# Attention step of a hybrid encoder layer: scores of a head pair as one group on eight PSUM banks, transposes in the pair's own step

## The chip, the cores and the metric

One NeuronCore of a Trainium2 chip. The time is the device time of the whole program in microseconds. The kernel before took 524.53 us (median of three runs, 524.23 to 525.28).

## What is computed

One encoder layer on 512 positions of width 1024. After an input projection one half of the mix is a gated linear recurrence, the other is attention with eight heads of 64 columns, and both are normed, projected out, and followed by an MLP. The change touches the attention:

```python
def dilated_attention(q, k, v, rel_bias):
    ...
        for offs, bias in pats:
            kpos = pos[:, None] + offs[None, :]
            ...
            logits = jnp.einsum('bqhd,bqjhd->bhqj', qb, kg).astype(jnp.float32) * scale
            logits = logits + bias[None, :, None, :]
            lse = jax.nn.logsumexp(logits, axis=-1)
            p = jnp.exp(logits - lse[..., None])
            outs.append(jnp.einsum('bhqj,bqjhd->bqhd', p.astype(v.dtype), vg).astype(jnp.float32))
            lses.append(lse)
        w = jax.nn.softmax(jnp.stack(lses, axis=0), axis=0)
        ...
        o = jnp.sum(w * jnp.stack(outs, axis=0), axis=0)
    ...
mix = jnp.concatenate([rms_norm(y_rnn, norm_rnn_g[l]), rms_norm(y_attn, norm_attn_g[l])], axis=-1)
x = x + mix @ w_out[l]
```

The kernel folds the three windows into one softmax: their multiplicities are logarithms inside the bias.

## The kernel before

Every float32 product is three products of split operands (`mm3`, lines 312 to 314), so a projection over 512 columns is one matmul after another with no pause. The program fixes the order on TensorE, ScalarE, VectorE and GpSimd by hand: an engine runs its instructions in the order in which the code emits them. SyncE (the queue SP) issues most transfers in order too; within the attention loop its order is also the code's.

The heads are worked in four pairs. For a pair and each of four query blocks `u`: `att_s` (line 806) makes the scores of both heads, each over 64 rows of the array, into one PSUM bank per head; `att_e` adds the bias and takes the minimum on VectorE (line 822; the bias windows `tw` are loaded by `load_tw`) and exponentiates on ScalarE (line 823); `att_t` transposes three 128x128 blocks per head and key block on TensorE (line 842) into a bank of the kind "et", which ScalarE copies out (line 845), and `att_c` transposes the small corner on VectorE. `att_z` takes the reciprocals of the row sums, writes them to DRAM (`zd`), and `att_zd` reads them back spread over 128 partitions (`zrow`). `att_av` (line 942) multiplies with the values over 64 columns of the array, and VectorE's `yp` (line 948) evacuates the sum, times `zrow`.

PSUM has eight banks: four "pj", two "gs", two "et". Between these pieces `fill(1)` emits one thunk: three matmuls of the query and key projections (`pqk`), later of the output projection (`pwo`). A thunk also carries the split of the next weights (`conv_hi`, line 247, `whi`; `conv_lo`, line 269, `wlo`, after which the next weight load `wraw` is issued). `beside` places side work by the table `plan`: the recurrence's end, norms, splits of queries and keys (`qh`, `kk`), and the sums and splits for the output projection (`osum`, `oh`, `ol`).

Before the change the loop has five steps `i` of four `u`. In step `i` the scores of pair `i` stand in two groups of 12 matmuls, and the transposes are those of pair `i - 1`; the value products stand at (2, 2) for pair 0, at (4, 0) for pairs 1 and 2, and behind the loop for pair 3. The step (4, 0) also loads the table for the square root (`act(warm, epsb, AF.Sqrt)`).

Of the kernel before, what the change touches and what calls it, by code (L numbers as in the profile page):

```python
# [17 lines left out]
P = 128  # L18
# [80 lines left out]
def hybrid_kernel(ctx: ExitStack, tc, xw0, xw, xn, w_in, w_v, w_out, w_up, w_dn, gates, vecs, bias, fg, out):  # L99
# [19 lines left out]
    def ps_(name, tag):  # L119
        return psum.tile([P, S], FT, name=name, tag=tag, bufs={"pj": 4, "gs": 2, "et": 2}[tag])  # L120
# [674 lines left out]
    QT = ((1, 0), (1, 1), (0, 0), (0, 1))  # L795
    QSEQ = (0, 3, 1, 2)

    def att_s(p, us):
        for u in us:
            psq[p, u] = [ps_("ps", "pj" if u % 2 else "gs") for _ in range(2)]  # L800
        for i, (a, b) in enumerate(((0, 0), (0, 1), (1, 0))):
            for u in us:
                qt = QSEQ[u]
                w = {(0, 0): TH + TH - WN, (0, 1): 0, (1, 0): TH - WN, (1, 1): TH}[QT[qt]]
                for e, r in enumerate(halves):
                    nc.tensor.matmul(psq[p, u][e][:, :NK], lhsT=qs_[p, a][r, P * qt:P * qt + P], rhs=kks[p][r, b, w:w + NK], start=i == 0, stop=i == 2)  # L806

    def att_e(p, u):
        qt = QSEQ[u]
# [71 lines left out]
    def att_y(p):  # L881
        y_add(1)
# [49 lines left out]

    def att_av(p, jts):
        if 0 in jts:
            pav[p] = ps_("pav", "gs" if p else "pj")
        for jt in jts:
            parts = av_parts(jt)
            for i, (ci, co) in enumerate(parts):
                for e in range(2):
                    a = slice(64 * e, 64 * e + 64)  # L940
                    h = 2 * p + e
                    nc.tensor.matmul(pav[p][a, co], lhsT=vs[:, jt, h * DH:(h + 1) * DH], rhs=et[h, jt][:, ci],  # L942
                                     start=jt == 0 and i == 0, stop=jt == 3 and i == len(parts) - 1, skip_group_check=True)
            for e in range(2):
                del et[2 * p + e, jt]
        if 3 in jts:
            y = g_("yp")
            nc.vector.tensor_tensor(y[:, ::-1], pav.pop(p), zrow.pop(p), op=OP.mult)
            yat[p] = y
            if p == 3:  # L950
                att_a(p)
            if p != 2:
                att_q(p)
            if p < 2:
                att_a(p)

    def att_q(p):
        y_sq(yat[p], 1)
# [1 line left out]
    def att_a(p):  # L960
        at[p] = g_("at")
        act(at[p], yat[p], AF.Copy, scale=vec("yg", 4 + p))
# [18 lines left out]
    def wo_thunks():  # L981
        order = [(0, tt, k) for tt in range(4) for k in range(4)] + [(1, tt, k) for h in (0, 2) for tt in range(4) for k in (h, h + 1)]
        pw = {}

        def end(n, tt):
            stt(x1[tt, n], pw[n, tt], rc[0][:, tt:tt + 1], x1[tt, n], op0=OP.mult, op1=OP.add)

        def mk(b, n, tt, k):
            def run():
                if k == 0:  # L990
                    pw[n, tt] = ps_("pwo", "pj")
                o = pw[n, tt]
# [7 lines left out]
                if n == 0 and tt and k == 1:  # L1000
                    end(0, tt - 1)
# [5 lines left out]
        st["wo"] = lambda tt: end(1, tt)  # L1007
        return [mk(b, *o) for b, o in enumerate(order)]

    KSPLIT = {7: s_hi, 8: s_lo}  # L1010
# [27 lines left out]
    def load_x():  # L1038
# [12 lines left out]
        def w_in(t, b):  # L1051
            return lambda: nc.sync.dma_start(t, oblock(b))
# [50 lines left out]
    def op(fn, *a):  # L1103
        return lambda: fn(*a)


    plan = {(0, 0, 0): [end(0)], (0, 0, 2): [sq_(0), add], (0, 0, 3): [end(1)],
            (0, 1, 1): [sq_(1)],
            (0, 2, 3): [add],
            (1, 0, 2): [end(2)],  # L1110
            (1, 1, 0): [sq_(2)], (1, 1, 2): [end(3)], (1, 1, 4): [add],
            (1, 3, 0): [sq_(3)], (1, 3, 2): [hi(0)], (1, 3, 3): [add, hi(1)], (2, 0, 2): [rnn_cols],
            (2, 0, 0): [lo(0), lo(1)], (2, 0, 4): [hi(2)],
            (2, 1, 2): [hi(3)], (2, 1, 4): [lo(2)], (2, 2, 3): [lo(3)]}
    for i in range(3):
        for key, (is_k, fn) in {(0, 2): (0, s_hi), (1, 0): (0, s_lo), (2, 2): (1, s_hi), (3, 0): (1, s_lo)}.items():
            plan.setdefault((i,) + key, []).append(lambda fn=fn, a=(i + 1, is_k): fn(*a))

    def beside(*key):
# [7 lines left out]
        fill(1)  # L1127
    assert not scans

    for key, fs in (((4, 1, 2), [(att_a, 2), (o_sum, "s1", 0), (o_sum, "s2", 0), (o_sum, "s3", 0), (o_sum, "s3", 1), (o_sum, "22", 0)]),  # L1130
                    ((4, 2, 0), [(o_hi, "s2", 0), (o_hi, "11", 0)]), ((4, 2, 2), [(o_lo, "s2", 0), (o_lo, "11", 0)]),
                    ((4, 3, 0), [(att_q, 2), (o_hi, "11", 1), (o_hi, "s3", 0), (o_hi, "s3", 1)]), ((4, 3, 2), [(o_lo, "11", 1), (o_lo, "s3", 0)]),
                    ((4, 3, 4), [(att_y, 2), (o_lo, "s3", 1), (o_hi2, 0), (o_hi, "s1", 0), (o_hi, "22", 0)])):
        plan[key] = [op(*a) for a in fs]
    FILL = {(3, 0): (1, 1, 1, 0), (3, 1): (1, 1, 1, 0), (3, 2): (1, 1, 1, 0), (4, 0): (0, 1, 0, 0), (4, 1): (0, 1, 0, 1), (4, 2): (0, 1, 0, 0), (4, 3): (0, 1, 0, 0)}


    AVS = {(2, 2): (0,), (4, 0): (1, 2)}
    with tc.manual_schedule(engines={nc.sync.engine}):
        for i in range(5):  # L1140
            for u in range(4):
                if i < 4:
                    if i == 2 and u == 2:
                        att_av(0, range(4))
                    if u % 2 == 0:
                        att_s(i, (u, u + 1))
                    if u == 2 and i < 3 or u == 0 and i:
                        for e in range(2):
                            load_tw(2 * (i + u // 2) + e, u // 2)
                if i >= 1:  # L1150
                    att_t(2 * i - 2, u)
                    att_t(2 * i - 1, u)
                if i < 4:
                    att_e(i, u)
                if i >= 1:
                    att_c(2 * i - 2, u)
                    att_c(2 * i - 1, u)
                if u == 0 and i >= 1:
                    att_z(i - 1)
                for p in AVS.get((i, u), ()) if i == 4 else ():  # L1160
                    att_av(p, range(4))
                if (i, u) == (4, 0):
                    act(warm, epsb, AF.Sqrt)
                beside(i, u, 0)
                fill(FILL.get((i, u), (1, 1, 1, 1))[0])
                beside(i, u, 1)
                fill(FILL.get((i, u), (1, 1, 1, 1))[1])
                if u == (1 if i == 4 else 2) and i >= 1:
                    att_zd(i - 1)
                for p in AVS.get((i, u), ()):  # L1170
                    if p != 2:
                        att_y(p)
                beside(i, u, 2)
                fill(FILL.get((i, u), (1, 1, 1, 1))[2])
                beside(i, u, 3)
                fill(FILL.get((i, u), (1, 1, 1, 1))[3])
                add_x()
                beside(i, u, 4)
    assert not plan and not more

    def load_t(half, n, f0):
        t = work.tile([P, 1024], FT, name="tw", tag="tw", bufs=4)
# [41 lines left out]
        nc.vector.tensor_tensor(hb["l"][k], hm[k], f(hb["h"])[:, k, :], op=OP.subtract)  # L1224

    fill(1)
    conv_lo(C_WA + 2)
    att_av(3, range(4))
    fill(1)
    o_sum("s1", 1)  # L1230
    o_sum("s2", 1)
    o_hi("s2", 1)
    remake(C_WA + OSEQ.index("s4"))
    fill(1)
    att_y(3)
# [13 lines left out]
    def rc_neg():  # L1249
        nc.vector.tensor_scalar(nrc, rc[1], -1.0, None, op0=OP.mult)  # L1250

    BES["11"].update({1: lambda: (o_lo("s2", 1), o_hi2(1), remake(C_WA + OSEQ.index("s1"))), 3: lambda: (rc_neg(), st["wo"](2))})
    BES["s2"].update({1: lambda: (o_lo2(0), conv_lo(C_WA + 3)), 2: lambda: o_hi("s1", 1), 3: lambda: (conv_lo(C_WA + 4), o_lo2(1))})
    BES["s3"][3] = lambda: (conv_lo(C_WA + 5), st["wo"](3))
# [570 lines left out]
```

## Time and profile before

| quantity | value |
|---|---|
| median of the runs | 524.53 us |
| the profiled execution | 524.5 us, its span 522.7 us |
| TensorE busy | 516.4 us, 99% |
| VectorE, ScalarE, GpSimd busy | 82%, 67%, 12% |

The profiled execution's span is 1.8 us shorter than its time; the prediction is made against its time. TensorE's granted clock is at full speed in all 40 slices. The chain that ended last is TensorE alone (99%). So a microsecond on TensorE, a pause or a slower stretch, is a microsecond of the kernel.

### The profile page before, as it was taken

The page shows a single profiled execution, that of the slowest core. Times are in us where ns is not written, and L with a number is a line of the kernel's source. Part 1 is how long each engine was busy: PE and PEld are TensorE (multiplying, and loading weights), DVE is VectorE, ACT ScalarE, POOL GpSimd, SP SyncE. Part 2 cuts the span into 40 slices and gives each one's busy share as a digit, 9 for nine tenths or more (in the row PEclk, how much of TensorE's full clock was granted, in tenths as well). Part 3 has the DMA queues.
Part 4 walks back from the last instruction along what each step waited for, and adds up shares of the span by engine and source line. Part 5 has one row for each costly group of instructions (what it writes and reads, how often), then busy time and mean ns, then how long its engine had stood idle before and what let it go on. Part 6 is the DMA issues. An engine that isn't in the chain of part 4 may idle for free.

```text
span 522.7 us, 8216 instructions
## 1 busy us (share of the span) xinstructions
PE 516.4 (99%) x3021; PEld 443.6 (85%) x3021; DVE 430.2 (82%) x667; ACT 352.7 (67%) x571; POOL 65.3 (12%) x89
## 2 busy tenths in 40 slices
PE   9999999999999999999999999999999999999995
PEld 7867888778787788899999888889999999888884
DVE  6999985788886898898789987789766977986985
ACT  7579946667857857586578656565667577655655
POOL 0183000000000321001300312001101300240000
PEclk9999999999999999999999999999999999999999
DMA  7736555267696499947695899976987497799804
GB/s 288 217 99 197 160 154 181 90 184 206 185 291 212 108 198 251 347 134 190 143 220 150 222 272 276 307 262 162 289 262 175 113 227 211 155 283 256 207 1 162
DMA packets 40329, 105.15 MB, mean 201 GB/s; under 512 B 5056, under 2 KB 13376, under 8 KB 40288
## 3 DMA queue, kind: packets, MB, share of 16 engines
q1 hardware_dynamic: 32448, 78.07, 45.1%
q0 software_dynamic: 7696, 26.32, 27.3%
q8 instruction: 24, 0.39, 0.3%
q10 hardware_dynamic: 144, 0.23, 0.1%
q14 instruction: 17, 0.14, 0.1%
HBM read 95.59 MB, written 4.29 MB: 191 GB/s over the span
## 4 chain that ended last, share of the span: by engine, by line
PE 99%; ACT 0%; DVE 0%; issue 0%
PE pu L314 10%; PE pu L312 10%; PE pu L313 10%; PE pd L314 10%; PE pd L313 10%; PE pd L312 10%; PE pqk L312 3%; PE pqk L313 3%; PE pqk L314 3%; PE pwo L312 3%; PE pwo L314 3%; PE pwo L313 3%; PE pav L942 2%; PE pt L842 2%; PE ps L806 2%; PE pp L312 1%
## 5 line engine op out<-in xcount | busy, mean ns | idle before, releaser
L269 DVE TENSOR_TENSOR wlo<-wraw,whi 128x1024 fp32r<-128x1024 f32 x71 | 86.6, 1220 | 24.3 <-ACT whi L247 24.1
L247 ACT ACTIVATE whi<-wraw 128x1024 fp32r<-128x1024 f32 x67 | 70.8, 1058 | 36.6 <-PE pd L314 18.2
L313 PE MATMUL pd<-wlo,ah 128*128 128x512 f32 (+1 forms) x195 | 75.2, 386 | 0.0
L312 PE MATMUL pd<-whi,ah 128*128 128x512 f32 (+1 forms) x195 | 75.2, 386 | 0.0
L314 PE MATMUL pd<-whi,al 128*128 128x512 f32 (+1 forms) x195 | 75.2, 386 | 0.0
L314 PE MATMUL pu<-hh,wlo 128*128 128x256 f32 x224 | 63.4, 283 | 0.0
L313 PE MATMUL pu<-hl,whi 128*128 128x256 f32 x224 | 63.4, 283 | 0.0
L312 PE MATMUL pu<-hh,whi 128*128 128x256 f32 x224 | 63.4, 283 | 0.0
L312 PE MATMUL pu<-h2h,whi 128*128 128x256 f32 (+1 forms) x200 | 60.1, 300 | 0.0
L313 PE MATMUL pu<-h2l,whi 128*128 128x256 f32 (+1 forms) x200 | 60.0, 300 | 0.0
L314 PE MATMUL pu<-h2h,wlo 128*128 128x256 f32 (+1 forms) x200 | 60.0, 300 | 0.0
L269 DVE TENSOR_TENSOR wlo<-tw,whi 128x1024 fp32r<-128x1024 f32 x37 | 45.2, 1221 | 16.8 <-ACT whi L247 16.8
L247 ACT ACTIVATE whi<-tw 128x1024 fp32r<-128x1024 f32 x38 | 40.1, 1059 | 24.7 <-PE pd L314 6.1
L247 ACT ACTIVATE whi<-ts 128x1024 fp32r<-128x1024 f32 x24 | 25.5, 1061 | 26.9 <-PE pd L314 18.7
L313 PEld LDWEIGHTS pu<-hl,whi 128*128 128x128 f32 x224 | 43.0, 192 | 0.0
L312 PEld LDWEIGHTS pu<-hh,whi 128*128 128x128 f32 x224 | 43.0, 192 | 0.0
L314 PEld LDWEIGHTS pu<-hh,wlo 128*128 128x128 f32 x224 | 43.0, 192 | 0.0
L313 PEld LDWEIGHTS pd<-wlo,ah 128*128 128x128 f32 x195 | 36.6, 188 | 7.4
L312 PEld LDWEIGHTS pd<-whi,ah 128*128 128x128 f32 x195 | 36.6, 188 | 7.4
L314 PEld LDWEIGHTS pd<-whi,al 128*128 128x128 f32 x195 | 36.6, 188 | 7.3
L313 PEld LDWEIGHTS pu<-h2l,whi 128*128 128x128 f32 x200 | 38.3, 191 | 1.3
L312 PEld LDWEIGHTS pu<-h2h,whi 128*128 128x128 f32 x200 | 38.3, 191 | 1.3
(283 smaller groups left out, 1219.0 us busy)
## 6 DMA issues: line engine op xcount, KB each, us to landing
wraw<-in_w_up_dram SPq DMA_DIRECT2D x25, 512.0 KB, 5.2
ts<-in_w_dn_dram POOLq DMA_DIRECT2D x24, 512.0 KB, 13.6
wraw<-in_w_dn_dram SPq DMA_DIRECT2D x24, 512.0 KB, 8.9
tw<-in_w_up_dram SPq DMA_DIRECT2D x15, 512.0 KB, 6.6
tw<-in_w_up_dram POOLq DMA_DIRECT2D x15, 512.0 KB, 7.7
wraw<-in_w_in_dram SPq DMA_DIRECT2D x13, 512.0 KB, 3.4
ts<-in_w_dn_dram SPq DMA_DIRECT2D x8, 512.0 KB, 8.2
tw<-in_w_dn_dram SPq DMA_DIRECT2D x8, 512.0 KB, 7.3
```

What stands on the lines that cost most here:

```text
L247: act(hi, raws[i], AF.Copy)
L269: nc.vector.tensor_tensor(lo, r, f(splits[i][0]), op=OP.subtract)
L312: nc.tensor.matmul(o, lhsT=a[0], rhs=b[0], start=bool(first), stop=False, skip_group_check=on)
L313: nc.tensor.matmul(o, lhsT=a[0], rhs=b[1], start=False, stop=False, skip_group_check=on)
L314: nc.tensor.matmul(o, lhsT=a[1], rhs=b[0], start=False, stop=bool(last), skip_group_check=on)
L806: nc.tensor.matmul(psq[p, u][e][:, :NK], lhsT=qs_[p, a][r, P * qt:P * qt + P], rhs=kks[p][r, b, w:w + NK], start=i == 0, stop=i == 2)
L842: nc.tensor.transpose(pt[:, i * P:(i + 1) * P], en[h][qt][:, k:k + P], ident)
L942: nc.tensor.matmul(pav[p][a, co], lhsT=vs[:, jt, h * DH:(h + 1) * DH], rhs=et[h, jt][:, ci], start=jt == 0 and i == 0, stop=jt == 3 and i ...
```

## The change

The loop now has four steps. Step `i` begins with the value products of pair `i - 1` and, behind them, all 24 score matmuls of pair `i` as one group: the four query blocks go to banks "pj", "gs", "et" and "pj", two each, so that the group takes all eight. The bias adds and exponentials of all four blocks follow in `u = 0`; the transposes of the same pair stand at `u = 2` and `u = 3`, two key blocks each, with two thunks (six projection matmuls) behind each block's transposes. `att_z` stands at `u = 2`, `att_zd` at `u = 3`, and the window loads of the next pair at `u = 0` and `u = 1`. Eight thunks instead of six stand ahead of the loop, and each place in the loop emits one. The table load for the square root stands at (3, 2). The table `plan` is new, and the first transfers for the output projection are regrouped.

```diff
-PRE = 6
+PRE = 8
...
-    def att_s(p, us):
-        for u in us:
-            psq[p, u] = [ps_("ps", "pj" if u % 2 else "gs") for _ in range(2)]
-        for i, (a, b) in enumerate(((0, 0), (0, 1), (1, 0))):
-            for u in us:
+    def att_s(p):
+        for u in range(4):
+            qt = QSEQ[u]
...
+            pss = psq[p, u] = [ps_("ps", ("pj", "gs", "et", "pj")[u]) for _ in range(2)]
+            for i, (a, b) in enumerate(((0, 0), (0, 1), (1, 0))):
...
-            pav[p] = ps_("pav", "gs" if p else "pj")
+            pav[p] = ps_("pav", "gs" if p == 3 else "pj")
...
-        w_in(b12, "12")()
         x_in(0, 0)()
-        more.append([x_in(1, 0)])
+        x_in(1, 0)()
+        more.append([w_in(b12, "12")])
...
-    AVS = {(2, 2): (0,), (4, 0): (1, 2)}
     with tc.manual_schedule(engines={nc.sync.engine}):
-        for i in range(5):
+        for i in range(4):
             for u in range(4):
...
+                beside(i, u, -1)
+                if u == 0:
+                    if i:
+                        att_av(i - 1, range(4))
+                    att_s(i)
+                    att_e(i, 0)
+                    att_e(i, 1)
+                if u > 1:
+                    turn(i, 2 * u - 4)
+                if u == 2:
+                    att_z(i)
+                beside(i, u, 0)
+                fill(1)
+                if u > 1:
+                    corner(i, 2 * u - 4)
+                if u == 3:
+                    att_zd(i)
+                beside(i, u, 1)
+                fill(1)
+                if u == 0:
+                    att_e(i, 2)
+                    att_e(i, 3)
+                if u == 1 and 1 <= i < 3:
+                    att_q(i - 1)
+                    att_a(i - 1)
+                if u > 1:
+                    turn(i, 2 * u - 3)
+                    corner(i, 2 * u - 3)
+                if (i, u) == (3, 2):
                     act(warm, epsb, AF.Sqrt)
+                if u < 2 and i < 3:
+                    for e in range(2):
+                        load_tw(2 * (i + 1) + e, 1 - u)
                 beside(i, u, 2)
+                fill(1)
...
```

`turn` is `att_t` for both heads of a pair, `corner` is `att_c` for both.

On TensorE, where pair 1's scores begin: `pqk` is a projection, `pt` the transposes, `pav` the value products, `ps` the scores. Before:

```order
L314 MATMUL pqk<-h_hi,wlo 128x512
L806 MATMUL ps<-kk,qh 128x416 x8
L806 MATMUL ps<-kk,ql 128x416 x4
L842 MATMUL pt<-ident,e 128x128 x6
L312 MATMUL pqk<-h_hi,whi 128x512
```

After:

```order
L941 MATMUL pav<-ett,vs 64x160 x2
L941 MATMUL pav<-ett,vs 64x416 x2
L805 MATMUL ps<-kk,qh 128x416 x4
L805 MATMUL ps<-kk,ql 128x416 x2
L805 MATMUL ps<-kk,qh 128x416 x4
L805 MATMUL ps<-kk,ql 128x416 x2
L805 MATMUL ps<-kk,qh 128x416 x4
L805 MATMUL ps<-kk,ql 128x416 x2
L805 MATMUL ps<-kk,qh 128x416 x4
L805 MATMUL ps<-kk,ql 128x416 x2
L312 MATMUL pqk<-h_hi,whi 128x512
```

The group has become 24 long, it stands behind value products, and a projection follows it in place of transposes. The whole program has 2933 matmuls on either side.

On ScalarE, step 1 of the change: the exponentials `e`, a weight split, a query split, two squares, `at` (the attention output times its gain), and then the copies of the first transposes.

```order
L822 ACTIVATE e,zz<-e,mn 128x416 x4
L247 ACTIVATE whi<-wraw 128x1024
L822 ACTIVATE e,zz<-e,mn 128x416 x4
L778 ACTIVATE qh<-qraw 128x512
L609 ACTIVATE ysq<-gt 128x512
L609 ACTIVATE ysq<-yp 128x512
L958 ACTIVATE at<-yp,vt 128x512
L844 ACTIVATE ett<-pt 128x384 x2
```

Before, two exponentials and two copies take turns through the whole step. In step 3 of the change, from the copies of the first two transposes on:

```order
L844 ACTIVATE ett<-pt 128x384 x4
L1174 ACT_TABLE_LOAD
L1174 ACTIVATE warm<-epsb 128x1
L247 ACTIVATE whi<-tw 128x1024
L897 ACTIVATE oh<-osum 128x256
L897 ACTIVATE oh<-at 128x256
L844 ACTIVATE ett<-pt 128x384 x4
```

Before, the table load stands between two copies (`L845`) with `ysq`, `at` and the value products of two pairs around it.

On SP, step 0 of the change: a weight load, four window pieces, the reciprocals out and back.

```order
L230 DMA wraw<-in_w_out_dram 128x1024
L476 DMA tw<-nbd 128x384
L478 DMA tw<-nbd 128x2x160
L476 DMA tw<-nbd 128x384
L478 DMA tw<-nbd 128x2x160
L873 DMA zd<-zt 4x32x32
L785 DMA kk<-kk 128x2x256
L878 DMA zrow<-zd 64x1x512 x2
```

Before, four further window pieces and a weight load stand between `zd` and `zrow`, and pair 0's `zrow` is not read until two steps later.

## Rows read from the trace of the kernel before

**Rows 1.** Part 1 of the page: busy time, share of the span, instructions

```profile
PE 516.4 (99%) x3021; PEld 443.6 (85%) x3021; DVE 430.2 (82%) x667; ACT 352.7 (67%) x571; POOL 65.3 (12%) x89
```

**Rows 2.** All waits of TensorE: total us, times, longest

```profile
PE pwarm L142 <- PEq L1814: 0.8, 1, 0.8
```

**Rows 3.** Timeline of TensorE, scores between projections: start us, us

```profile
100.19 0.39 PE L313 MATMUL pqk<-h_lo,whi 128*128 128x512 f32 x1
100.42 0.39 PE L314 MATMUL pqk<-h_hi,wlo 128*128 128x512 f32 x1
100.74 1.02 PE L806 MATMUL ps<-kk,qh 64*128 64x416 f32 x8
...
102.40 0.40 PE L313 MATMUL pqk<-h_lo,whi 128*128 128x512 f32 x1
```

**Rows 4.** The same, scores and then transposes, between two projections

```profile
107.45 0.39 PE L314 MATMUL pqk<-h_hi,wlo 128*128 128x512 f32 x1
...
110.04 0.40 PE L313 MATMUL pqk<-h_lo,whi 128*128 128x512 f32 x1
```

**Rows 5.** The same, transposes alone with six projection matmuls between them

```profile
165.27 0.39 PE L314 MATMUL pwo<-whi,yl 128*128 128x512 f32 x1
165.50 0.82 PE L842 MATMUL pt<-ident,e 128*128 128x128 f32 x6
...
166.39 0.39 PE L313 MATMUL pwo<-wlo,yh 128*128 128x512 f32 x1
...
167.54 0.81 PE L842 MATMUL pt<-ident,e 128*128 128x128 f32 x6
```

**Rows 6.** The same, one pair's value products

```profile
132.56 3.02 PE L942 MATMUL pav<-ett,vs 128*64 128x416 f32 x24
```

**Rows 7.** Timeline of ScalarE, a run without idle time

```profile
104.50 0.63 ACT L778 ACTIVATE kk<-kraw 128x512 fp32r<-128x512 f32 x1 [0.50 <-DVE kraw L765]
105.03 1.05 ACT L247 ACTIVATE whi<-wraw 128x1024 fp32r<-128x1024 f32 x1
105.98 0.63 ACT L823 ACTIVATE e<-e,mn 128x416 f32<-128x416 f32 x1
...
106.61 0.63 ACT L823 ACTIVATE e<-e,mn 128x416 f32<-128x416 f32 x1
```

**Rows 8.** Timeline of ScalarE around the table load

```profile
163.33 0.71 ACT L962 ACTIVATE at<-yp,vt 128x512 f32<-128x512 f32 x1
164.06 1.28 ACT L1163 ACT_TABLE_LOAD   x1
...
166.09 0.87 ACT L845 ACTIVATE ett<-pt 128x384 f32<-128x384 f32 x2 [0.53 <-PE pt L842]
...
168.82 0.42 ACT L898 ACTIVATE oh<-osum 128x256 fp32r<-128x256 f32 x1
...
169.47 0.87 ACT L845 ACTIVATE ett<-pt 128x384 f32<-128x384 f32 x2
```

**Rows 9.** Timeline of VectorE, an evacuation and the first bias add behind it

```profile
135.97 0.69 DVE L948 TENSOR_TENSOR yp<-pav,zrow 128x512 f32<-128x512 f32 x1
136.76 0.59 DVE L822 CUSTOM_DVE_ANT_0 e<-ps,tw 128x416 f32<-128x416 f32 x1
```

**Rows 10.** Timeline of SP's issues, two stretches

```profile
126.39 0.33 SPq L230 DMA_DIRECT2D wraw<-in_w_out_dram  x1
...
128.76 0.59 SPq L874 DMA_DIRECT2D zd<-zt  x1
...
162.15 0.58 SPq L874 DMA_DIRECT2D zd<-zt  x1
...
164.21 1.17 SPq L879 DMA_DIRECT2D zrow<-zd  x2
```

**Rows 11.** Transfers from 88 to 180 us: KB each, median us to landing

```profile
tw<-nbd SPq DMA_DIRECT2D x12, 160.0 KB, 5.3
```

**Rows 12.** The reads of zrow, from issue to landing

```profile
DMA to landing us min/median/max: 3.0/4.6/5.4
```

More of the change, by code (lines that the diff above doesn't have):

```diff
@@ L796, in hybrid_kernel @@
     QSEQ = (0, 3, 1, 2)
[L798 to L804 removed]
+    def att_s(p):
+        for u in range(4):
+            qt = QSEQ[u]
+            w = {(0, 0): TH + TH - WN, (0, 1): 0, (1, 0): TH - WN, (1, 1): TH}[QT[qt]]
+            pss = psq[p, u] = [ps_("ps", ("pj", "gs", "et", "pj")[u]) for _ in range(2)]
+            for i, (a, b) in enumerate(((0, 0), (0, 1), (1, 0))):
                 for e, r in enumerate(halves):
[L806 removed]
+                    nc.tensor.matmul(pss[e][:, :NK], lhsT=qs_[p, a][r, P * qt:P * qt + P], rhs=kks[p][r, b, w:w + NK], start=i == 0, stop=i == 2)
     def att_e(p, u):
@@ L999, in run @@
                     conv_lo(C_WO + {3: 3, 17: 4, 20: 5}[b])
-                if n == 0 and tt and k == 1:
-                    end(0, tt - 1)
+                if n == 0 and (tt, k) == (3, 1):
+                    end(0, 2)
                 if n and (tt, k) == (0, 1):
@@ L1006, in mk @@
             return run
-        st["wo"] = lambda tt: end(1, tt)
+        st["wo"] = end
         return [mk(b, *o) for b, o in enumerate(order)]
@@ L1104, in op, with ends @@
         return lambda: fn(*a)
[L1107 to L1114, printed above, removed]
+    def ends():
+        st["wo"](0, 0)
+        st["wo"](0, 1)
+    plan = {(0, 0, 2): [end(0)], (0, 1, 0): [sq_(0), end(1)], (0, 1, 3): [add], (0, 2, 1): [sq_(1)], (0, 3, 2): [add],
+            (1, 0, -1): [end(2)], (1, 1, 0): [sq_(2)], (1, 2, 0): [end(3)], (1, 2, 1): [add], (1, 2, 2): [sq_(3), hi(0)],
+            (1, 3, 1): [hi(1)], (1, 3, 3): [add, hi(2)], (1, 3, 4): [hi(3)],
+            (2, 0, -1): [lo(0), lo(1), lo(2)], (2, 1, 0): [lo(3)], (2, 2, 2): [rnn_cols],
+            (3, 0, -1): [ends]}
     for i in range(3):
-        for key, (is_k, fn) in {(0, 2): (0, s_hi), (1, 0): (0, s_lo), (2, 2): (1, s_hi), (3, 0): (1, s_lo)}.items():
+        for key, (is_k, fn) in {(0, 2): (0, s_hi), (2, 0): (0, s_lo), (2, 2): (1, s_hi), (3, 0): (1, s_lo)}.items():
             plan.setdefault((i,) + key, []).append(lambda fn=fn, a=(i + 1, is_k): fn(*a))
@@ L1128, in hybrid_kernel @@
     assert not scans
[L1130 to L1134, printed above, removed]
@@ L1135, in hybrid_kernel @@
-    FILL = {(3, 0): (1, 1, 1, 0), (3, 1): (1, 1, 1, 0), (3, 2): (1, 1, 1, 0), (4, 0): (0, 1, 0, 0), (4, 1): (0, 1, 0, 1), (4, 2): (0, 1, 0, 0), (4, 3): (0, 1, 0, 0)}
-    AVS = {(2, 2): (0,), (4, 0): (1, 2)}
+    for key, fs in (((3, 1, 0), [(att_a, 2)]),
+                    ((3, 1, 4), [(o_sum, "s1", 0), (o_sum, "s2", 0)]), ((3, 2, 2), [(o_sum, "s3", 0), (o_sum, "s3", 1), (o_sum, "22", 0)]),
+                    ((3, 2, 3), [(o_hi, "s2", 0), (o_hi, "11", 0)]), ((3, 3, 0), [(o_lo, "s2", 0), (o_lo, "11", 0)]),
+                    ((3, 3, 2), [(att_q, 2), (o_hi, "11", 1), (o_hi, "s3", 0), (o_hi, "s3", 1)]), ((3, 3, 3), [(o_lo, "11", 1), (o_lo, "s3", 0)]),
+                    ((3, 3, 4), [(att_y, 2), (o_lo, "s3", 1), (o_hi2, 0), (o_hi, "s1", 0), (o_hi, "22", 0)])):
+        plan.setdefault(key, []).extend(op(*a) for a in fs)
@@ L1139, in hybrid_kernel, with turn, corner @@
+    def turn(p, jt):
+        for e in range(2):
+            att_t(2 * p + e, jt)
+    def corner(p, jt):
+        for e in range(2):
+            att_c(2 * p + e, jt)
     with tc.manual_schedule(engines={nc.sync.engine}):
-        for i in range(5):
+        for i in range(4):
             for u in range(4):
[L1142 to L1162, printed above, removed]
-                    act(warm, epsb, AF.Sqrt)
[L1164 to L1172, printed above, removed]
@@ new lines, in hybrid_kernel @@
+                beside(i, u, 1)
[10 more added lines that the diff above has]
+                if (i, u) == (3, 2):
+                    act(warm, epsb, AF.Sqrt)
+                if u < 2 and i < 3:
+                    for e in range(2):
+                        load_tw(2 * (i + 1) + e, 1 - u)
@@ L1173, in hybrid_kernel @@
                 beside(i, u, 2)
-                fill(FILL.get((i, u), (1, 1, 1, 1))[2])
+                fill(1)
+                if u == 3 and 1 <= i < 3:
+                    att_y(i - 1)
                 beside(i, u, 3)
-                fill(FILL.get((i, u), (1, 1, 1, 1))[3])
+                fill(1)
                 add_x()
                 beside(i, u, 4)
-    assert not plan and not more
+    assert not plan
     def load_t(half, n, f0):
@@ L1226, in hybrid_kernel @@
     fill(1)
+    add_x()
     conv_lo(C_WA + 2)
@@ L1229, in hybrid_kernel @@
     fill(1)
+    add_x()
     o_sum("s1", 1)
@@ L1232, in hybrid_kernel @@
     o_hi("s2", 1)
+    add_x()
+    assert not more
     remake(C_WA + OSEQ.index("s4"))
```

7 lines of the change are left out of this document (2 added, 5 removed).

## The prediction

> **What bounds the kernel now.** I read the busy times first: TensorE is busy 516.4 of 522.7 us [rows 1], and the list of its waits holds one entry, 0.8 us at the start [rows 2]. So nothing that VectorE, ScalarE or a transfer does costs time today, and the work of TensorE is the same before and after: 2933 matmuls of the same shapes. The change can gain only where TensorE's rhythm is uneven, and it loses wherever it makes TensorE wait for the first time. Both are read from starts in TensorE's timeline; busy time cannot show the first, since neighbouring matmuls overlap.
>
> **What it removes: changes of tile shape.** Projections follow each other every 0.23 us (100.19 to 100.42) [rows 3]. From the last start ahead of a score group to the second projection behind it pass 1.98 us (100.42 to 102.40) [rows 3]. Without a pause it would be six pairs of scores at 0.23 x 416/512 = 0.187, 1.12 us, and two projections, 0.45: 1.57. So a score group costs 0.41 us more than its work, 0.20 for going over to half the rows and 0.20 for coming back. Where transposes follow the scores, the stretch is 2.59 us (107.45 to 110.04) [rows 4]; six transposes between projections alone take 1.12 (165.27 to 166.39) [rows 5], the scores 1.12, so 0.35 is left: 0.20 for going over, 0.15 for coming back.
>
> Before, I count 21 changes between full tiles, score tiles and value-product tiles: eight score groups have 16 ends, six of them before transposes; the value products have three beginnings and two ends of their own. After: four groups of scores, three of them joined to value products: 13 changes, none from scores to transposes. Eight are saved, six of 0.15 and two of 0.20: 1.3 us. That the value products cost as much per change as the scores isn't in a row of its own; at 0.15 for all it is 1.2, at 0.20 for all 1.6. I take **-1.3 us**, bounds 1.2 to 1.6.
>
> **What it adds, first place: step 3, behind the table load.** The "et" banks are two, and a turn of transposes fills both, so it waits for ScalarE's copies of the turn before. Let T be the start of the second turn of step 3. Turns come every 2.04 us with six projections between (165.50 to 167.54) [rows 5]; the fourth turn is due at T + 4.08. ScalarE starts the second turn's copies at T + 0.59 (165.50 [rows 5] to 166.09 [rows 8]); two take 0.87, and neighbours on ScalarE overlap by 0.1 (105.03 + 1.05 to 105.98 [rows 7]), so it is free at T + 1.35. In the new order there stand ahead of the third turn's copies: the table load 1.28 [rows 8], a short warm-up (0.1 at the least), a weight split 0.95 (105.03 to 105.98) [rows 7], two conversions `oh` 0.65 (168.82 to 169.47) [rows 8]. That is T + 4.33; the first copy frees its bank 0.49 later (two in 0.87 with 0.1 shared), T + 4.8. TensorE waits 0.75, some 0.1 more for the semaphore and the second bank: **+0.9 us**. Before, the load had value products of two pairs beside it, and ScalarE even sat idle behind it, 0.53 us [rows 8]; that cover is gone. Bounds: 0.6, if the weight split gets ahead of the load's end in part, to 1.0.
>
> **Second place: step 1, `zrow` and the chain behind it.** G is the start of pair 1's scores, when the value products of pair 0 have just ended. VectorE evacuates them (`yp`), which needs `zrow`, and everything on VectorE stands behind: the eight bias adds, and through them ScalarE. Let `yp` start at Y. The first exponential follows at Y + 1.25 (`yp` 0.69 and a bias add 0.59 [rows 9], shared 0.1, a hand-over). On ScalarE then stand eight exponentials at 0.63 (105.98 to 106.61), a weight split 0.95, `qh` and two squares at 0.53 (104.50 to 105.03) [rows 7], `at` 0.62 (0.71 [rows 8] less 0.1): 8.2 us. The first copy of the first turn is done at Y + 9.95. TensorE comes to the second turn at G + 10.05: 24 scores 2.45 (12 x 0.187 and a change), 24 projections 5.45, a change 0.1, a turn with its projections 2.04. So the wait is about Y - G, and 0.1 again where the next copies follow. If `zrow` is there, Y - G is 0.1, and the place costs 0.2.
>
> When does `zrow` land? It is now read in the next step, where pair 0 had two steps before. TensorE starts pair 0's first turn 11.2 us ahead of G (four turns at 2.04, a change, value products 3.02 [rows 6]). VectorE has the split that frees the next weight buffer at about that place, so SP issues `wraw` some 0.8 us later, G - 10.4, then four window pieces and `zd`, 2.37 behind the weight load (126.39 to 128.76) [rows 10]: G - 8.0. `zd` alone lands within 2.06 us (162.15, until the read behind it is issued at 164.21) [rows 10]. But it is queued behind the windows, which take 5.3 [rows 11]. I take 5.2. `zrow` is two issues, the second 0.6 later, and lands in 3.0 to 5.4 [rows 12]; the queue is nearly empty by then, as it was in the shortest, so 3.1. That gives G - 8.0 + 5.2 + 0.6 + 3.1 = G + 0.9, and **+0.9 us** for the place. Bounds: `zrow` in time, 0.2; `zrow` at its median 4.6 behind 5.3, 2.5.
>
> **What is taken at nothing, and its cover.** The scores' last bank is the one that `yp` empties: TensorE comes to it at G + 1.85, `yp` ends at Y + 0.75, so at Y = G + 0.9 there is 0.2 of cover, and each tenth of lateness past 1.1 is then paid there instead. The next projection needs the first score bank, free at Y + 1.2 and wanted at G + 2.45: 0.35 of cover. Step 2 has the same chain on ScalarE with one square less, step 3 with no square and no query split, so ScalarE is 0.5 us or more ahead there; step 2's `zd` stands behind windows too, but TensorE comes 0.9 later after the wait of step 1, and step 3's has none straight ahead. The two more thunks ahead of the loop and the new places of the recurrence's end, norms and splits are work of ScalarE and VectorE, idle 33% and 18% of the span [rows 1]; where a chain of them comes to TensorE is what the two places are about. The output projection's transfers start later, since the buffers that they overwrite are held until the last query or key projection; their first reader is ten and more projections away. The MLP and the tail are the same instructions.
>
> **Sum**, against the profiled execution's 524.5 us (the median of the runs is 524.53): 524.5 - 1.3 + 0.9 + 0.9 = 525.0; with 0.1 for hand-overs in the two waits that I did not count, 525.1. That is no change that can be told: 0.2%, 1.05 us, is about what a measurement of this kernel can tell from none.
>
> **A rule that speaks against it.** The table load takes 1.28 us and starts 0.02 us after the operation before it, 163.33 + 0.71 [rows 8]: no pause is seen. The Trainium skill (ScalarE: Activation LUTs, What ACT_TABLE_LOAD costs) says that a switch costs a drain of about 1.38 us besides the load, 2.66 in all. By the load alone the first place costs 0.9 us, by that rule 2.3 and the kernel would take 526.5; the trace doesn't agree.
>
> **The rivals.**
> - *The waits don't come about: faster.* Both waits are sums of ScalarE's queue against TensorE's; if ScalarE's copies were in time in both places, 524.5 - 1.3 = 523.2. For it: TensorE waits nowhere today with the same operations on ScalarE [rows 2]. Against it: the table load's place has 0.75 us too little by plain addition, with no transfer in it. 0.08.
> - *`zrow` in time, the table load's wait alone:* 524.5 - 1.3 + 0.9 + 0.2 = 524.3, no change. It needs `zd` and `zrow` together 0.8 us quicker. 0.16.
> - *`zrow` late, slower.* The round trip through DRAM decides; at Y - G of 1.4 and more the sum passes 525.55. At 2.5 it is 524.5 - 1.3 + 0.9 + 2.5 = 526.6, and a like delay at step 3, where a weight load and `kk` stand ahead of `zrow`, would add to it. For it: half of the reads so far took 4.6 us or more [rows 12]. Against: no window is issued between `zd` and `zrow` now. 0.23.
> - *A pause ahead of the table load, as the rule has it:* 526.5, slower. Only the rule speaks for it. 0.03.
>
> **How the numbers follow.** Forecast as summed, 524.6 to 525.55: 0.50. With the second rival, within 0.2%: 0.66. Slower 0.26, faster 0.08. The range leaves out the first rival and the far end of the third: the low end is 524.5 - 1.6 + 0.6 + 0.2 = 523.7; the high end 524.5 - 1.2 + 1.0 + 2.5 = 526.8.
>
> **What would show it.** In TensorE's waits: two new entries, `pt` waiting for ScalarE's `ett`, one of 0.8 to 1.0 us in step 3 (behind the table load), one of some 0.8 in step 1; perhaps `ps` waiting for `yp`. VectorE idle before pair 0's `yp`, ended by the `zrow` transfer, some 0.8 us. Scores to be started every 0.19 us in a run of 24, with about 0.2 at each end. It would be wrong if consecutive scores into one bank were slower than into four in turn (24 scores over 2.6 us), if `zrow` lands more than 1 us off, or if a wait shows up on a weight split of the output projection, whose buffers come free later.

## The result: 1 us up in the median, hardly more than can be told, from two full waits and a small one

The changed kernel takes 525.51 us (median of 15 runs, 524.96 to 526.32) against 524.53; the ratio is 1.0019, 95% interval 1.0012 to 1.0026: clear of 1, and astride the 0.2% that the prediction took as the least that can be told. The profiled execution has a span of 523.8 us against 522.7. TensorE is as busy as before [rows 1]:

```profile
PE 516.3 (99%) x3021; PEld 444.4 (85%) x3021; DVE 430.4 (82%) x667; ACT 351.4 (67%) x571; POOL 66.2 (13%) x89
```

All waits of TensorE, after (before, only the first was there [rows 2]):

```profile
PE pwarm L142 <- PEq L1825: 0.8, 1, 0.8
PE pt L841 <- ACT ett L844: 0.7, 1, 0.7
PE ps L805 <- DVE yp L947: 0.6, 1, 0.6
```

Where they stand is read from TensorE's timeline: step 0's scores, which wait for nothing, then step 1's second turn, step 3's scores, and step 3's third and fourth turns, the third without a wait.

```profile
95.30 0.64 PE L805 MATMUL ps<-kk,qh 64*128 64x416 f32 x4
...
97.76 0.50 PE L312 MATMUL pqk<-h_hi,whi 128*128 128x512 f32 x1
...
124.39 0.39 PE L314 MATMUL pqk<-h_hi,wlo 128*128 128x512 f32 x1
124.70 0.92 PE L841 MATMUL pt<-ident,e 128*128 128x128 f32 x6
125.38 0.48 PE L312 MATMUL pqk<-h_hi,whi 128*128 128x512 f32 x1
...
153.24 0.65 PE L805 MATMUL ps<-kk,qh 64*128 64x416 f32 x4
...
155.94 0.64 PE L805 MATMUL ps<-kk,qh 64*128 64x416 f32 x3 [0.55 <-DVE yp L947]
...
156.69 0.50 PE L312 MATMUL pwo<-whi,yh 128*128 128x512 f32 x1
...
166.32 0.82 PE L841 MATMUL pt<-ident,e 128*128 128x128 f32 x6
166.89 0.48 PE L312 MATMUL pwo<-whi,yh 128*128 128x512 f32 x1
...
168.13 0.39 PE L314 MATMUL pwo<-whi,yl 128*128 128x512 f32 x1
169.19 0.93 PE L841 MATMUL pt<-ident,e 128*128 128x128 f32 x6 [0.67 <-ACT ett L844]
169.88 0.48 PE L312 MATMUL pwo<-whi,yh 128*128 128x512 f32 x1
```

A stretch is priced by its starts. A turn without a wait starts 0.23 behind the projection ahead of it [rows 5] and hands over to the next after 0.57 (166.32 to 166.89). The fourth turn took 1.06 and 0.69: **0.95 us**. The second turn of step 1 took 0.31 and 0.68: **0.19**, too little for the list of waits. A group of 24 scores takes 2.46 in step 0 (95.30 to 97.76) and 3.45 in step 3 (153.24 to 156.69): **0.98**. Together 2.1 us.

The gain is read over the attention, from the first query projection to the last pair's value products, two rows of TensorE's timeline. Before:

```profile
78.67 0.39 PE L312 MATMUL pqk<-h_hi,whi 128*128 128x512 f32 x1
171.02 3.02 PE L942 MATMUL pav<-ett,vs 128*64 128x416 f32 x24
```

After:

```profile
78.89 0.39 PE L312 MATMUL pqk<-h_hi,whi 128*128 128x512 f32 x1
172.12 3.02 PE L941 MATMUL pav<-ett,vs 128*64 128x416 f32 x24
```

92.35 us have become 93.23, with the same number of matmuls of each kind between the two rows: 0.88 more, although 2.1 us of waits were added. So some 1.2 us were saved.

What made step 3 wait is on SP and VectorE. SP's issues around two round trips of `zrow` (step 0 for pair 0, step 2 for pair 2):

```profile
106.54 0.66 SPq L873 DMA_DIRECT2D zd<-zt  x1
108.23 0.64 SPq L785 DMA_DIRECT2D kk<-kk  x1
110.70 1.20 SPq L878 DMA_DIRECT2D zrow<-zd  x2
...
141.15 0.49 SPq L230 DMA_DIRECT2D wraw<-in_w_up_dram  x1
143.47 0.59 SPq L873 DMA_DIRECT2D zd<-zt  x1
144.15 1.01 SPq L1045 DMA_DIRECT2D x<-in_xn_dram  x2
145.21 0.68 SPq L1048 DMA_DIRECT2D ws<-in_w_out_dram  x1
148.05 0.33 SPq L230 DMA_DIRECT2D wraw<-in_w_up_dram  x1
148.65 0.65 SPq L785 DMA_DIRECT2D kk<-kk  x1
149.39 1.20 SPq L878 DMA_DIRECT2D zrow<-zd  x2
```

VectorE's `yp` of the same pairs, in steps 1 and 3:

```profile
114.67 0.69 DVE L947 TENSOR_TENSOR yp<-pav,zrow 128x512 f32<-128x512 f32 x1 [0.97 <-PE pav L941]
...
155.19 0.69 DVE L947 TENSOR_TENSOR yp<-pav,zrow 128x512 f32<-128x512 f32 x1 [3.83 <-PE ps L805]
```

In step 1 `yp` starts 0.14 behind the value products (G is 114.53). In step 3 it starts 1.95 behind them, and what the row names as releaser, the scores, is nothing that `yp` reads; what it reads is `zrow`, issued at 149.39 and 0.6 later. All reads of `zrow` whose landing the view of the tile can tell, from issue to landing:

```profile
DMA to landing us min/median/max: 2.6/2.8/5.5
```

Each transfer by itself is read from the trace's semaphore updates: it has landed with the last of its own. In step 0 `zd` landed at 110.68, 4.1 us behind its issue, SP issued the reads at once, and they took 2.6 and 2.8. In step 2 `zd` landed at 148.94, after 5.5 us, the reads went out 0.45 later, behind `kk`, and took 5.5 and 5.1 (154.85 and 155.07). Both halves of the round trip were long.

### The profile page after: what moved, and what is told of

Its sections match the earlier page's. It is cut to its first block, busy times and chain, and to the rows that moved or that the text cites. A ratio compares the mean times of both kernels' runs of the same rounds, so it can differ in the third digit from the quotient of the medians.

```text
span 523.8 us, 8225 instructions
## 1 busy us (share of the span) xinstructions
PE 516.3 (99%) x3021; PEld 444.4 (85%) x3021; DVE 430.4 (82%) x667; ACT 351.4 (67%) x571; POOL 66.2 (13%) x89
## 4 chain that ended last, share of the span: by engine, by line
PE 98%; ACT 1%; DVE 0%; issue 0%
PE pu L314 10%; PE pu L312 10%; PE pu L313 10%; PE pd L314 10%; PE pd L312 10%; PE pd L313 10%; PE pqk L312 3%; PE pqk L314 3%; PE pqk L313 3%; PE pwo L312 3%; PE pwo L314 2%; PE pwo L313 2%; PE pav L941 2%; PE ps L805 2%; PE pt L841 2%; PE pp L312 1%
## 5 line engine op out<-in xcount | busy, mean ns | idle before, releaser
L314 PEld LDWEIGHTS pu<-h2h,wlo 128*128 128x128 f32 x200 | 38.3, 191 | 1.3
```

The source lines that it names most:

```text
L314: nc.tensor.matmul(o, lhsT=a[1], rhs=b[0], start=False, stop=bool(last), skip_group_check=on)
```

## The experiments

**Table load behind the last turn.**

```diff
-                if (i, u) == (3, 2):
+                if (i, u) == (3, 3):
                     act(warm, epsb, AF.Sqrt)
```

> The Sqrt table load stands one place later, behind the copies of step 3's last turn instead of those of its second but last step; nothing else is changed. In the changed kernel TensorE's fourth turn of step 3 starts 0.83 us late (169.19, where the sixth projection before it would have let it start at 168.36), with about 0.1 more lost in and behind the turn. Theory A (this wait is the table load's, paid in full): the wait is gone, 525.5 - 0.9 = 524.6 us. Rival B (ScalarE is behind anyway from the late zrow of the step's beginning, or the load only moves the wait to the weight splits and conversions of the output projection behind it): a wait of some 0.8 us shows up on a projection after 172 us, and the time stays at 525.5. Rival C (the load takes a pause besides its 1.28 us): 1.4 us more ScalarE time behind the last turn would also meet the split wlo/whi there; 525.9 or more.

526.02 us, ratio 1.0029 (1.0018 to 1.0041): by its mechanism rival B, but the new wait is 1.3 us, not 0.8, and the time 0.5 longer, as rival C had it. C's pause is not there: the load starts 0.02 us behind the copy ahead of it and takes 1.28. In TensorE's waits the `pt` entry is gone and a longer one has come:

```profile
PE pwo L312 <- DVE x L1215: 1.3, 1, 1.3
...
PE ps L805 <- DVE yp L947: 0.7, 1, 0.7
```

The load now delays the split `whi`, on it VectorE's `wlo`, and behind that stand the last `yp` and the norm chain that ends in `x`, which frees a bank of the output projection (VectorE's timeline):

```profile
175.24 1.22 DVE L269 TENSOR_TENSOR wlo<-ws,whi 128x1024 fp32r<-128x1024 f32 x1
176.38 0.68 DVE L947 TENSOR_TENSOR yp<-pav,zrow 128x512 f32<-128x512 f32 x1
...
182.81 0.75 DVE L1215 SCALAR_TENSOR_TENSOR x<-pwo,rcy,x 128x512 f32<-128x512 f32 x1
```

In the changed kernel that `yp` starts at 175.39, 3.3 us behind the start of the last value products (172.12); here 4.9 behind it (171.52). TensorE's last output projection starts 30.2 us behind them, not 28.6: of 1.6 us of delay all is paid, so the chain has next to no cover. A wait removed by putting its cause ahead of another tight chain is only moved.

**`zrow` ahead of `kk` in step 2.**

```diff
+                if (i, u) == (2, 3):
+                    att_zd(i)
                 beside(i, u, 0)
...
-                if u == 3:
+                if u == 3 and i != 2:
                     att_zd(i)
```

> In step 2 alone, the two reads of zrow are issued one projection earlier, ahead of the weight load and the copy of kk on SP's queue, which wait for VectorE. In the changed kernel they are issued at 149.39 and land 5.3 us later, TensorE having come to the scores at 153.24 and waiting at their last bank. Theory A (zrow is late because it is issued behind kk, which waits until 148.65): issue about 2 us earlier, at some 147.2, landing at 152.5, yp starts at once, no wait of ps on yp, 525.5 - 1.0 = 524.5 us. Rival B (the transfers of the output projection ahead of it on the DMA engines set the landing, whenever it is issued): zrow lands at 154.7 as before and the wait of ps stays within 0.2 us, 525.4. Rival C (kk, now behind zrow, comes late for the scores): a new wait of ps on the kk transfer; 525.5 or more.

525.16 us, 1.0016 (1.0008 to 1.0025): rival C by its mechanism, though 0.35 below the changed kernel. SP reads `zrow` at 148.69, when `zd` has landed (148.63); `kk` now stands behind a 512 KB load:

```profile
148.69 1.17 SPq L878 DMA_DIRECT2D zrow<-zd  x2
149.97 0.53 SPq L230 DMA_DIRECT2D wraw<-in_w_up_dram  x1
150.59 0.64 SPq L785 DMA_DIRECT2D kk<-kk  x1
```

TensorE waits for `kk` inside the scores, which comes 5.3 us after its issue:

```profile
156.08 0.65 PE L805 MATMUL ps<-kk,qh 64*128 64x416 f32 x4 [1.27 <-DMA kk<-kk]
```

The two reads took 3.3 and 3.9 us by their semaphore updates, although loads follow them, and `yp` starts right behind the value products. The profiled execution took 526.39, 1.2 above the median, so its wait for `kk` is longer than most: by the medians it costs some 0.6 (an estimate, 0.98 less 0.35).

**Both edits.** Nothing else differs.

> Both of these edits. Theory A (two independent waits, both paid in full): 525.5 - 0.9 - 1.0 = 523.6 us, 0.9 below the kernel before, and TensorE's waits hold no pt or ps entry over 0.2 us. Rival B (ScalarE or VectorE is the bound of step 3, and the two waits are one shortage shown in two places): removing both gains no more than one, 524.5.

525.87 us, 1.0028 (1.0017 to 1.0040): the two new waits side by side, 1.3 us for `x` and 1.2 for `kk`. Neither theory, since each edit had only put one wait in place of another.

**Both edits, score groups split.**

```diff
-                    att_s(i)
+                    att_s(i, (0, 1))
+                    fill(1)
+                    att_s(i, (2, 3))
...
-                fill(1)
+                if u:
+                    fill(1)
```

> Both edits as in the run before, and the score group of each step is split into two halves with one projection (three matmuls) between them, taken from those that followed: four groups more with two ends each, the same 2933 matmuls. It prices the first term of the prediction by itself. Theory A (a change of tile shape costs TensorE about 0.2 us): 8 x 0.2 = 1.6 us more than the run before, 525.2 if that gives 523.6; the first score of each half and the projection behind it show a start about 0.1 us later than inside a group. Rival B (the joined groups are not what saved time; a change costs nothing or is hidden): the time of the run before, 523.6.

527.16 us (5 runs), 1.0047 (1.0034 to 1.0061). It prices nothing cleanly: the projection between gives `kk` time, so the wait for `kk` goes as the changes of shape come. It was made again below.

**Table load between the first two turns.**

```diff
+                if (i, u) == (3, 2):
+                    act(warm, epsb, AF.Sqrt)
                 if u == 2:
                     att_z(i)
...
-                if (i, u) == (3, 2):
-                    act(warm, epsb, AF.Sqrt)
```

> The Sqrt table load stands one turn earlier than in the changed kernel: between the copies of step 3's first and second turns, where ScalarE sat idle 0.88 us. Worked out from the changed kernel's rows: load and warm-up end at 165.2 instead of 167.1, the third turn's copies start at 167.5 instead of 168.67, their first bank is free at 168.0 and TensorE comes at 168.36. Theory A (TensorE's wait is what stands on ScalarE between two turns, and the later place of the first experiment lost because the load then stood ahead of the chain that ends the last pair: split, yp, norm, Sqrt, x): no pt wait, everything behind 0.9 us earlier including that chain, no pwo wait, 525.5 - 0.9 = 524.6 us. Rival B (the chain behind the last pair's value products is bound elsewhere, by transfers or by VectorE, so that it comes no earlier): the pt wait goes and a pwo wait on x of about 0.6 us comes, 525.2.

524.55 us, 0.9999 (0.9991 to 1.0008): theory A, 1.0 less than the changed kernel, and neither a `pt` nor a `pwo` wait. ScalarE, with the third turn's copies at 167.43 (167.5 was worked out):

```profile
163.72 1.28 ACT L1155 ACT_TABLE_LOAD   x1
...
165.13 0.85 ACT L844 ACTIVATE ett<-pt 128x384 f32<-128x384 f32 x2
...
167.43 0.87 ACT L844 ACTIVATE ett<-pt 128x384 f32<-128x384 f32 x2
```

**One load of 512 KB from ahead of `zrow` to behind it.**

```diff
-                add_x()
+                for _ in range({(2, 2): 0, (2, 3): 2}.get((i, u), 1)):
+                    add_x()
```

> The first weight load of the output projection's second half (ws, 512 KB) is issued one place later, behind zrow instead of 4.2 us ahead of it; zrow and kk stay where they are in the changed kernel. Theory A (zrow, and kk where zrow was put ahead of it, came late because half a megabyte and more was ahead of them on the DMA engines, 99% busy at some 370 GB/s): 512 KB fewer are 1.4 us at that rate; zrow lands 3.9 us after its issue instead of 5.3, yp starts about 0.5 us behind the value products, inside the scores' cover, no ps wait; 525.5 - 1.0 = 524.5 us. Rival B (loads issued behind zrow slow it as much as those ahead, since the engines share between them): landing at 5 us and more, the ps wait stays at 0.5 or more, 525.3. Rival C (what the held load feeds comes late): a wait of DVE or a projection on ws, over 525.5.

524.99 us, 1.0006 (0.9997 to 1.0015): less than theory A asked. The reads took 5.2 and 4.8 us, not 3.9, step 3's scores 3.16 us in place of 3.45, and `yp` waits openly for the transfer:

```profile
154.48 0.69 DVE L947 TENSOR_TENSOR yp<-pav,zrow 128x512 f32<-128x512 f32 x1 [3.75 <-DMA zrow<-zd]
```

The load taken away had been issued 4 us before the read; the `wraw` (512 KB) and `kk` (256 KB) that are issued at most 1.3 us ahead of it stayed. `zd` still took 5.0 us, so this load, issued behind it, is not what made it late. Why 512 KB fewer gave 0.3 us and not the 1.4 that was expected stays open: in the changed kernel that load landed at 151.78, behind the reads' issue.

**These two and a square taken ahead of step 1's exponentials.**

```diff
-            (1, 0, -1): [end(2)], (1, 1, 0): [sq_(2)], ...
+            (1, 0, -1): [end(2), sq_(2)], ...
```

> The two edits before together, and the third square of the recurrence's output taken ahead of step 1's exponentials (ScalarE sat idle 5.19 us there), which was one of the operations ahead of the first turn's copies. Theory A (three independent waits of 0.94, 1.0 and 0.2 us): 525.5 - 2.1 = 523.4 us, 1.1 below the kernel before, and no wait in TensorE's list but the one at the start; that is what the fewer changes of tile shape give alone. Rival B (the next chain, that of the last pair's norm, has little cover and takes most of it back): a pwo wait on x, 524.2 or more.

524.16 us, 0.9996 (0.9987 to 1.0005). Between the two theories: the turns of step 1 and step 3 run without a wait, step 3's scores still take 2.99 us (153.26 to 156.25), 0.5 more than without one, and at the bank that `x` frees TensorE loses under 0.1.

**`zrow` behind a weight load in step 0.** `att_zd(0)` is called at the end of step 0.

> In step 0 alone, the two reads of zrow are issued after the weight load behind them, some 1.7 us later than in the changed kernel. It tries the price that the prediction put on a late zrow in step 1. Worked out: issues at 112.6 and 113.2, landing 2.8 us later at 116.0, 1.45 us behind the value products' end at 114.5. Theory A (each tenth past 1.1 is paid at the scores' last bank, the rest at the second turn through ScalarE's queue): the two waits together 1.4 us, against 0.2 in the changed kernel, 525.5 + 1.2 = 526.7 us. Rival B (ScalarE's idle time ahead of the exponentials, 5.19 us, is slack that the lateness eats): no more than the wait at the scores, 0.35 to 0.45, 525.9.

525.73 us, 1.0023 (1.0014 to 1.0031). It says nothing on the price, since `zrow` did not come late: the reads went out at 110.00, 4.0 behind `zd` (4.2 in the changed kernel), with the weight load now in the time that SP had waited. What holds the reads in this step is the landing of `zd`, not what stands ahead of them on SP.

**Step 2's transfers cleared.** The edits of the second and sixth experiment, and the loop and the code behind it under one written order for SP, so that the MLP's weight loads stay behind the last value products.

```diff
-    assert not plan
+        assert not plan
...
-    conv_lo(C_WA + 2)
-    att_av(3, range(4))
+        conv_lo(C_WA + 2)
+        att_av(3, range(4))
```

> Against the changed kernel, step 2's transfers are put in another order, and nothing else: zrow is read ahead of the copy of kk (as in the second experiment), the first ws load is issued behind both (as in the sixth), and the weight loads of the MLP, which SP's queue drew forward to between them (wraw, 512 KB, issued at 148.05 in the changed kernel), stay behind the last pair's value products. So SP comes to zrow as soon as zd has landed, and 1 MB fewer stands ahead of zrow and kk. Theory A (the wait of step 3's scores is made of both: what stands ahead on the DMA engines, and what SP waits for): zrow issued at 147.7 to 148.7 and landed by 152, kk issued at 148.7 and landed by 152.5, TensorE at the scores at 153.2: no ps wait, 525.5 - 1.0 = 524.5 us. Rival B (zrow and kk take 4.5 us and more behind one another whatever stands ahead): a ps wait of 0.3 us or more, on yp or on kk. Rival C (the MLP's loads are wanted earlier): a new wait behind 199 us.

524.39 us, 1.0000 (0.9991 to 1.0009): theory A. The only wait left in TensorE's list is the fourth turn's; step 3's scores take 2.47 us. Both of the MLP's loads are gone from step 2, the one ahead of `zd` as well (141.15 in the changed kernel). On SP, `zd` lands in 3.1 us and `kk` is issued 1.8 earlier than in the second experiment, counted from each profile's first query projection:

```profile
142.86 0.59 SPq L873 DMA_DIRECT2D zd<-zt  x1
...
146.06 1.18 SPq L878 DMA_DIRECT2D zrow<-zd  x2
148.05 0.64 SPq L785 DMA_DIRECT2D kk<-kk  x1
```

By their semaphore updates the reads took 2.6 and 2.8 us, and `kk` 2.5.

**All edits.** The run before, the table load of the fifth experiment and the square of the seventh.

> The run before and the two edits of ScalarE's order (the table load between the first two turns of step 3, the square ahead of step 1's exponentials). Theory A (the three waits of 0.94, 0.2 and 1.0 us are all there is beside the tile shapes): no wait but the one at the start; from the seventh run's profile, where 0.36 us was left at step 3's scores, 524.2 - 0.35 = 523.8 us, and about 0.15% below the kernel before. Rival B (the norm's chain behind the last pair, whose cover was used up to within 0.1 us in the seventh run, sets the end): TensorE waits at the output projection for x by what the step 3 wait gave, and the time stays at 524.2.

**523.39 us, 0.9980 (0.9971 to 0.9989)**: 1.1 us below the kernel before, 2.1 below the changed one. All of TensorE's waits:

```profile
PE pwarm L142 <- PEq L1828: 0.8, 1, 0.8
```

The attention's first and last row:

```profile
78.63 0.39 PE L312 MATMUL pqk<-h_hi,whi 128*128 128x512 f32 x1
169.75 3.02 PE L941 MATMUL pav<-ett,vs 128*64 128x416 f32 x24
```

91.12 us: 2.11 less than the changed kernel, the sum of the three waits (0.95 + 0.19 + 0.98), and 1.23 less than before, with no wait left in it: what the tile shapes give alone.

**`zd` behind `kk` in step 0.**

```diff
-                if u == 2:
+                if u == 2 and i:
                     att_z(i)
...
                 if u == 3:
+                    if i == 0:
+                        att_z(i)
                     att_zd(i)
```

> Against the changed kernel, in step 0 alone zd is written one place later on SP's queue, behind kk instead of ahead of it (108.9 instead of 106.54), so that its landing, for which the reads of zrow wait, is later too: what the eighth experiment did not reach. It tries the price that the prediction put on a late zrow in step 1. If zd takes 4.1 us as before, the reads go at 113.0 and land at 116.4, Y - G = 1.85; if zd takes 2.1 behind nothing, 114.4 and Y at 114.7 at the latest, no change. Theory A (the two waits of step 1 together are Y - G + 0.1, past 1.1 at the scores' last bank, the rest at the second turn): 1.9 us at Y - G of 1.85, against 0.2 now, 525.5 + 1.7 = 527.2; in general 525.4 + Y - G. Rival B (only the wait at the scores is paid; ScalarE makes up the rest in its idle time): 0.85 at Y - G of 1.85, 526.3.

525.89 us, 1.0022 (1.0013 to 1.0030). `zd` went out 2.4 later but landed in 2.9, so that `yp` came only 0.46 behind the value products (G is 114.52). VectorE:

```profile
114.98 0.69 DVE L947 TENSOR_TENSOR yp<-pav,zrow 128x512 f32<-128x512 f32 x1 [1.29 <-DMA zrow<-zd]
```

TensorE's second turn of step 1:

```profile
124.36 0.39 PE L314 MATMUL pqk<-h_hi,wlo 128*128 128x512 f32 x1
124.88 0.92 PE L841 MATMUL pt<-ident,e 128*128 128x128 f32 x6
125.55 0.48 PE L312 MATMUL pqk<-h_hi,whi 128*128 128x512 f32 x1
```

The second turn now costs 0.29 + 0.10 = 0.39 us, 0.20 more for 0.32 of lateness. The other 0.12 lies beside the scores, since the first bias add waits for its scores as well: it starts 0.73 behind `yp` in the changed kernel, 0.60 here. So theory A's price holds roughly at this small size (by its rule 0.56 in all at a lateness of 0.46, and 0.39 was paid), and rival B does not: no wait at the scores of step 1 is paid and the turn pays. The time itself can't check it, since step 3 moved as well in this profile: its two reads took 5.8 and 5.4 us, and its scores 3.84 in place of 3.45. A lateness of 1 us and more in step 1 was not reached.

**All edits, score groups split.** The split of the fourth experiment on the run in which TensorE waits nowhere.

> The run with all edits, in which TensorE waits nowhere after the start, with each step's score group split into two halves by one projection, as in the fourth experiment, which could not price this since its waits changed too. Eight ends of score groups more, the same 2933 matmuls. Theory A (each end costs 0.2 us, and nothing else differs): 4 x 0.41 = 1.6 us, 523.4 + 1.6 = 525.0 us, ratio to the kernel before 1.001. Rival B (the joined groups are not what makes that run faster than the kernel before): 523.4, ratio 0.998.

525.22 us, 1.0013 (1.0004 to 1.0022): theory A. First and last row of the attention:

```profile
78.96 0.39 PE L312 MATMUL pqk<-h_hi,whi 128*128 128x512 f32 x1
...
171.67 3.02 PE L941 MATMUL pav<-ett,vs 128*64 128x416 f32 x24
```

92.71 us, 1.59 more for eight ends of score groups: 0.20 each. (This profile has a wait of 0.5 us at 7.9 us, ahead of the attention; none in it.) So the grouping by itself has the price that the prediction gave it, and it is enough for the whole gain of 1.23: with these eight ends put back the attention is 0.36 longer than before.

## Why the prediction came out, and which step failed

525.1 was forecast and 525.5 came. Two steps were off in opposite directions, one by 0.7 us and one by 1.0, so that the total came out so near is luck.

- **Changes of tile shape, -1.3:** -1.23, from the run without waits, and 0.20 per end of a score group by the split alone. The mechanism and the size hold; a run of 24 scores into eight banks keeps the pace of 0.187 a pair.
- **First place, the table load, +0.9:** +0.95. The third turn's copies were worked out for T + 4.33; T is 164.28 and they started at 168.67, T + 4.39. The load starts 0.02 us behind the copy ahead of it, and moving it by one turn takes the whole wait away. No pause like the one that the Trainium skill gives (ScalarE: Activation LUTs, What ACT_TABLE_LOAD costs) is seen at this load in any of these runs; by it the kernel would have taken 526.5.
- **Second place, `zrow` in step 1, +0.9:** +0.19, and this is the first step that was off. SP wrote `zd` at G - 8.0, as worked out. But 5.2 was taken for its landing, from the window pieces ahead of it; the reads went out after 4.2, and landed within 2.8 instead of 3.1. So `zrow` was there in time, and the place cost the 0.2 that was given for that case. What a late `zrow` costs here was tried at a lateness of 0.46 alone, where 0.39 of the forecast 0.56 was paid.
- **Step 3's `zrow`, taken at nothing, +0.98:** the step that failed. The text said that "step 3's has none straight ahead", and looked only at windows. Ahead of `zd` stands a weight load of the MLP that SP's queue draws forward, 512 KB, issued 2.3 us before it, and `zd` took 5.5 us to land. Ahead of the reads stand a second such load and `kk`, 256 KB; `kk` held the reads 0.45 us more, to 149.39, and they then took 5.5 and 5.1. With the reads ahead of the second load and `kk` they took 3.3 and 3.9 and `kk` paid; with both loads gone `zd` took 3.1, the reads 2.6 and 2.8, and nobody waited. The third rival named "a like delay at step 3, where a weight load and `kk` stand ahead of `zrow`", as an addition to a late step 1; it came alone. The cover was as worked out: at a lateness of 1.95, 0.85 past the 1.1 of cover, and 0.1 for starting again.
- **The rest at nothing:** right but for the norm chain behind the last pair, which the text did not weigh. Its cover is so thin that it took back more than the gain of the first experiment.

By the measured terms: 524.5 - 1.23 + 0.95 + 0.19 + 0.98 = 525.4, and 0.1 behind the attention, where the output projection's last matmul starts 28.5 us behind those value products before and 28.6 after. Of the rivals, "`zrow` in time, the table load's wait alone" was right for step 1, and "`zrow` late" for step 3. That the loads ahead of `zd`, `zrow`'s issue time and the loads ahead of `zrow` were changed together in the run that cleared step 2 leaves their shares open: at 146.06 + 0.6 + 5.3 = 152.0 the reads would have been in time for step 3's scores at 152.6 even at the old landing time, by the earlier `zd` alone.

The Trainium skill (DMA: Bandwidth & Descriptors, Queues, rings and completion order) says that each DMA engine consumes a ring's descriptors in ring order. The traces agree: in the changed kernel `wraw`, `kk` and the reads of `zrow`, issued in this order, landed at 153.37, 154.25, 154.85 and 155.07; in the second experiment the reads, `wraw` and `kk`, issued in that order, at 152.00, 153.12, 155.25 and 155.94. The small `zd` alone came ahead of the load issued before it, at 148.94 against 149.17 in the changed kernel.

## What to carry to other kernels

Where TensorE is the bound, count the ends of groups of another tile shape in the starts of its timeline, not in busy time; each has a price (here 0.2 us), and joining groups is worth that times their number. But a reordering that joins them also takes cover from chains that were hidden, so follow each value that TensorE's next bank needs back to its transfer, for every step of the loop by itself: the step in which another phase's loads begin is not like the others. When a wait is removed, look at the next chain behind it before the place of the cause is chosen. And when a transfer is late, time each part of its round trip by itself: a median over all reads hid that both the write and the read were slow in one step.

## What the runs showed of the hardware

How long a small round trip through DRAM takes depends on what has been issued ahead of it on the same queue: in step 2 `zd` (16 KB) landed after 5.5 us with a 512 KB load issued 2.3 us ahead of it and after 3.1 without that load, and `zrow` (128 KB a read) after 5.1 and 5.5 behind 768 KB just issued and 2.6 and 2.8 without. Over the changed kernel and its twelve variants `zd` took 2.4 to 5.9 us and a read of `zrow` 2.4 to 5.8. TensorE's first query projection started between 78.29 and 79.12 us in the fourteen profiles, though nothing ahead of it was changed on TensorE: profiles of single executions differ by 0.8 us before the change is reached, so differences were taken over stretches and not over spans.
